# One two-bank tile for the scores of both attention halves, and three banks each for the other two groups

## The chip, the core and the metric

The kernel runs on one core of a Trainium2 chip. The metric is the device time of one execution in microseconds (us), lower is better. A profile of one execution is read beside it: TensorE is PE (its weight loads PEld), VectorE is DVE, ScalarE is ACT, GpSimd is POOL, and SP issues most transfers. L147 is line 147 of the kernel before.

## What is computed

One decoder block over 1024 tokens of width 1024 in float32. The part that the change touches is the sliding-window attention with sinks: 8 query heads and 2 key/value heads of width 64, blocks of 128 queries against the previous and their own 128 keys.

```python
s = jnp.einsum('bnqhgd,bnkhd->bnhgqk', qb, kk).astype(jnp.float32) * scale
...
s = jnp.where(valid[None, :, None, None], s, NEG_INF)
...
p = jax.nn.softmax(jnp.concatenate([s, sink], axis=-1), axis=-1)[..., :-1]
o = jnp.einsum('bnhgqk,bnkhd->bnqhgd', p.astype(v.dtype), vv)
```

Around it stand an input norm and projection (pool input, queries, keys, values, gates), a multi-scale pooling branch, gated merging, an output projection, and a squared-ReLU MLP with sandwich norms. The later stages are not changed.

## The kernel before

**Precision.** Each float32 operand is split into a high and a low part (`split`, L97: a cast on ACT at L98, a subtraction at L99, mostly on DVE), and each product is three matmuls: high x high, high x low, low x high (`PASSES`).

**Stages on PE, in order of time.** First the projections of queries, keys and values for token tiles 0 to 3, as x and the weights arrive (`mm_q` L147, `mm_kv` L153). Then eight one-column matmuls (L201) that end the sum of squares for the norm. Then the attention stage, tile by tile (n = 0 to 7): `qkv_tile(n + 4)` projects a later tile, 24 matmuls of 512 columns and 24 of 256; `pre_qkv` (L221, L222, on DVE) empties its banks, and rotates; `post_qkv` transposes queries and keys (L239, L240) and splits them; `score(n, g)` makes the scores of four heads; `attend(n, g)` makes their softmax, transposes it (L300), splits it (tiles "pt") and multiplies with the values (L307). Then the pooling branch: `pool_u` (48 matmuls of 512 columns for each of four groups, L345 and L347), `pool_in` on DVE, `pool_mix` (L518 to L520, evacuated at L521). Then the gates (`Pairs`, L408), and everything after.

**Scores.** In `score` the two key/value heads are two halves of 64 partitions each. Each of the 12 matmuls of a group (n, g) uses one half, so 64 of the 128 rows of PE. Each half has its own PSUM tile. Four reductions on DVE (L275) mask the scores and take their maxima.

**PSUM.** There are eight banks. One pool holds them in two groups of four, by tag: "at" (projections of tiles 0 and 1 at the start, transpositions, scores, products with the values) and "mm" (projections, pool_u, gates). All later stages use the same two tags.

**Order.** The engines run their instructions in the order that is built into the program. A scheduler makes that order when the program is built: by priority, which is by default the order in the source, and by whether a free buffer of the tag is there. So the projections of `qkv_tile` and the matmuls of `pool_u` stand between the steps of the attention.

Of the kernel before, what the change touches and what calls it, by code (L numbers as in the profile page):

```python
# [8 lines left out]
F32 = mybir.dt.float32  # L9
F32R = mybir.dt.float32r  # L10
AF = mybir.ActivationFunctionType
ALU = mybir.AluOpType
AX = mybir.AxisListType

P = 128
# [3 lines left out]
NK = D // P  # L19
# [4 lines left out]
HD = 64  # L24
# [7 lines left out]
PASSES = ((0, 0), (0, 1), (1, 0))  # L32
# [18 lines left out]
def block_kernel(ctx: ExitStack, tc, xt, x, consts, vecs, sinks, b_qkv, g_post, g_mlp, g_mlp_post,  # L51
                 w_qkv, w_u, w_g, w_pool, w_bp, w_ba, w_o, w_up, w_dn, x1_dram, spill, f_dram, out):
    nc = tc.nc
    act, dve, pool, pe = nc.scalar, nc.vector, nc.gpsimd, nc.tensor
# [3 lines left out]
    st = ctx.enter_context(tc.tile_pool(name="st", bufs=3))  # L58
    wp = ctx.enter_context(tc.tile_pool(name="wp", bufs=6))
    sp = ctx.enter_context(tc.tile_pool(name="sp", bufs=3))  # L60
    ps = ctx.enter_context(tc.tile_pool(name="ps", bufs=4, space=bass.MemoryType.PSUM))

    z_dram, y_dram, yp_dram = (spill[i:j] for i, j in ((0, 16), (16, 20), (20, 24)))
    cnt = [0]
# [1 line left out]
    def nm(s):  # L66
        cnt[0] += 1
        return f"{s}_{cnt[0]}"
# [13 lines left out]
    def at(tag, bufs, shape, dt=F32):  # L82
        return ap_.tile([P] + shape, dt, tag=tag, name=nm(tag), bufs=bufs)

    def bank(tag, shape=None):
        return ps.tile([P] + (shape or [512]), F32, tag=tag, name=nm(tag))

    def small(n=8, tag="sm"):
        return sp.tile([P, n], F32, tag=tag, name=nm(tag))
# [4 lines left out]
    def f32(ap):  # L94
        return ap.bitcast(F32)

    def split(hi, lo, src, eng=dve):  # L97
        act.copy(hi, src)  # L98
        eng.tensor_tensor(lo, src, f32(hi), ALU.subtract)  # L99
# [22 lines left out]
    nsnk = cp.tile([P, NH], F32, name="nsnk")  # L122
# [27 lines left out]
    def mm_kv(n, k, joint=False):  # L150

        for j, (xh, h) in enumerate(PASSES):
            pe.matmul(bkv[n // 2 * 2][:, n % 2, :], xs_[k][n // 4][:, xh, n % 4 * P:(n % 4 + 1) * P],  # L153
                      wkv[k // 2][:, h, k % 2, :], start=k == 0 and j == 0 and not (joint and n % 2),
                      stop=k == NK - 1 and j == 2 and not (joint and n % 2 == 0))

    bq = {0: bank("at"), 1: bank("at"), 2: bank("mm"), 3: bank("mm")}
    bkv = {0: bank("at", [2, 256]), 2: bank("mm", [2, 256])}
    bss = bank("at", [NT])
    sq = at("qkv", 2, [S])  # L160
    ones = vec[:, V_ONE:V_ONE + 1]
    for k in range(NK):
# [14 lines left out]
        kv = wkv[-1]  # L177
# [27 lines left out]
    khi = at("khi", 1, [S], F32R)  # L205
    klo = at("klo", 1, [S], F32R)
# [27 lines left out]
    def post_qkv(n):  # L234
        tf = tfs.pop(n)
        t = tf[:, :768].rearrange("p (h d) -> p h d", d=HD)
        bt, bk = bank("at"), bank("at")
        for m in range(4):
            pe.transpose(bt[:, m * P:(m + 1) * P], tf[:, m * P:(m + 1) * P], ident)  # L239
        pe.transpose(bk[:, :P], tf[:, 512:640], ident)  # L240
        qt = at("qt", 2, [2, 512], F32R)
        split(qt[:, 0, :], qt[:, 1, :], bt)
        ks = slice(n * P, (n + 1) * P)
        split(khi[:, ks], klo[:, ks], bk[:, :P])
        vt = at("v", 4, [2, 3, HD], F32R)
        pool.memset(f32(vt[:, :, 1, :]), 0.0)
        split(vt[:, 0, ::2, :], vt[:, 1, ::2, :], t[:, 10:12, :], pool)
        vs[n] = vt.rearrange("p l a d -> p l (a d)")
        qts[n] = qt
# [3 lines left out]
    def score(n, g):  # L253
        qt = qts[n]
        k0 = max(n - 1, 0) * P
        nk = 2 * P if n else P
        msk = mask[:, 2 * P - nk:]
        s4 = at("s4", 4, [4, 256])
        if g == 0:
            soft[n] = tuple(sp.tile([P, NH], F32, tag=t, name=nm(t)) for t in ("nmx", "es", "den"))  # L260
        nmx = soft[n][0]
        sb = [bank("at", [2, 256]) for _ in range(2)]
        for i in range(2):
            m = 2 * g + i
            for j, (qx, kx) in enumerate(((0, khi), (0, klo), (1, khi))):
                for kv in range(2):
                    r = slice(kv * HD, (kv + 1) * HD)
                    pe.matmul(sb[kv][:, i, :nk], qt[r, qx, m * P:(m + 1) * P], kx[r, k0:k0 + nk],  # L268
                              start=j == 0, stop=j == 2)

        for i in range(2):
            for kv in range(2):
                j = 2 * i + kv
                h = 4 * g + j
                dve.tensor_tensor_reduce(s4[:, j, :nk], sb[kv][:, i, :nk], msk, -HD ** -0.5, nsnk[:, h:h + 1],  # L275
                                         ALU.add, ALU.min, nmx[:, h:h + 1])
        scores[n, g] = s4

# [43 lines left out]
    rb = bcp.tile([P, 1024], F32, tag="bc", name="rb_all")  # L322
# [10 lines left out]
    def load_w(src, shape):  # L333
        ws = stage(shape)
        nc.sync.dma_start(ws, src)
        hi, lo = wslot(shape), wslot(shape)
        split(hi, lo, ws)
        return hi, lo

    def mm_fm(bs, whi, wlo, rhs, nk):  # L340

        for k in range(nk):
            for th in range(2):
                for hl in range(2):
                    pe.matmul(bs[th], whi[:, k, :], rhs(k, hl, th), start=k == 0 and hl == 0, stop=False)  # L345
            for th in range(2):
                pe.matmul(bs[th], wlo[:, k, :], rhs(k, 0, th), start=False, stop=k == nk - 1)  # L347

    def xr(k, hl, th):
        return xs_[k][th][:, hl, :]  # L350
# [96 lines left out]
    pre_qkv(0)  # L447
    pre_qkv(1)
    post_qkv(0)
    score(0, 0)  # L450
    score(0, 1)
    post_qkv(1)
    pre_qkv(2)
    pre_qkv(3)
    for n in range(NT):
        if n + 4 < NT:
            qkv_tile(n + 4)
        if n:
            score(n, 1)
        attend(n, 0)  # L460
        if n + 1 < NT:
            score(n + 1, 0)
        attend(n, 1)
        if n % 4 == 3:
            for kh in range(2):
                nc.sync.dma_start(y_dram[n // 4 * 2 + kh], flat(y[n // 4][kh]))
        if n == 1:
            make_rb()
        if n + 2 < NT:
            post_qkv(n + 2)  # L470
        if n + 4 < NT:
            pre_qkv(n + 4)
    us = {}

    def pool_u(gi):
        whi, wlo = load_w(w_u[gi], [NK, P])
        bs = [bank("mm"), bank("mm")]
        mm_fm(bs, whi, wlo, xr, NK)
        u = ga_.tile([P, S], F32, tag="ga", name=nm("u"))
        for th in range(2):  # L480
            sl = slice(th * 512, (th + 1) * 512)
            dve.tensor_tensor(u[:, sl], bs[th], rb[:, sl], ALU.mult)
        act.activation(u, u, AF.Identity, bias=vec[:, V_BU + gi:V_BU + gi + 1])
        us[gi] = u

# [10 lines left out]
    def pool_in(gi):  # L496
        w = WINDOWS[gi]
        u = us[gi]
        src, step = u, 1
        while step < w:  # L500
            t = flat(yy.tile([P, 2, 512], F32, tag="y", name=nm("t")))
            dve.tensor_tensor(t[:, step:], src[:, step:], src[:, :S - step], ALU.add)
            dve.tensor_copy(t[:, :step], src[:, :step])
            src, step = t, 2 * step
        dve.scalar_tensor_tensor(u[:, w - 1:], src[:, w - 1:], 1.0 / w, u[:, w - 1:], ALU.mult, ALU.subtract)
        dve.tensor_tensor(src[:, :w - 1], src[:, :w - 1], cst[:, C_CNT:C_CNT + w - 1], ALU.mult)
        dve.tensor_tensor(u[:, :w - 1], src[:, :w - 1], u[:, :w - 1], ALU.subtract)
        dhi, dlo = ar([S]), ar([S])
        split(dhi, dlo, u)
        d[gi] = dhi, dlo  # L510

    def pool_mix(gi):
# [9 lines left out]
        nc.scalar.dma_start(yp_dram[gi], yt)  # L522

    pool_u(3)
    pool_in(3)
    pool_u(2)
    pool_u(1)
    pool_mix(3)
    pool_in(2)
# [2 lines left out]
    pool_in(1)  # L532
    pool_in(0)
    ap_pool.__exit__(None, None, None)
    gp_pool = tc.tile_pool(name="gp", bufs=17, reuse_waits="tile")
    gp = gp_pool.__enter__()

# [84 lines left out]
    for p in range(8):  # L622
# [4 lines left out]
        tag = "at" if p % 2 == 0 else "mm"  # L627
# [276 lines left out]
    for p in range(1, NP):  # L904
# [3 lines left out]
        tag = "at" if p % 2 == 0 else "mm"  # L908
# [29 lines left out]
    def acc4(name):  # L938
        return [dl.tile([P, 512], F32, tag="acc", name=nm(name), bufs=16) for _ in range(4)]
# [82 lines left out]
    u, v, c11, c12 = acc4("u"), acc4("v"), acc4("c11"), acc4("c12")  # L1022
# [5 lines left out]
    for j, (i, s_) in enumerate(steps):  # L1028
        if j + AHEAD < len(steps):
            operands(*steps[j + AHEAD])  # L1030
        if s_ == 0 and i not in (2, 3):
            tag = "mm" if i in (5, 7) else "at"
            banks[i] = [bank(tag) for _ in range(4)]
        bs = banks[{2: 1, 3: 5}.get(i, i)]
# [104 lines left out]
```

## Time and profile before

| | us |
|---|---|
| three runs | 1170.08, 1171.26, 1171.52 |
| median | 1171.26 |
| the profiled execution, its own time | 1171.98 |
| its span | 1170.2 |
| PE busy | 1142.4 (98%) |
| DVE busy | 828.2 (71%) |
| ACT busy | 533.9 (46%) |

A row of matmuls gives their count, their busy time, and the mean length of one in ns. Matmuls are pipelined, so lengths overlap: what one costs is the busy time over the count, or the distance of two starts. The chain of waits follows the work that ended last back to its releasers. In the timeline the figure in brackets is the idle time of the engine before the row and what ended it.

### The profile page before, as it was taken

How to read it: one execution, taken by the hardware profiler on the slowest of the kernel's cores; microseconds unless marked ns; L12 is line 12 of the kernel's file. 1: busy time of each engine (PE TensorE's matmuls, PEld its weight loads, DVE VectorE, ACT ScalarE, POOL GpSimd, SP SyncE). 2: the span in 40 equal slices, each digit the busy share in tenths (PEclk: the TensorE clock that was granted, in tenths of full speed). 3: DMA queues.
4: the chain of work that ended last, by engine and by line, in shares of the span. 5: the costliest groups of instructions: out<-in, count | busy, mean ns of one | idle time of the engine just before them, and what ended most of it. 6: DMA issues, size and time to landing. Idle time of an engine off the chain costs nothing.

```text
span 1170.2 us, 14371 instructions
## 1 busy us (share of the span) xinstructions
PE 1142.4 (98%) x5356; PEld 942.4 (81%) x5356; DVE 828.2 (71%) x1337; ACT 533.9 (46%) x926; POOL 53.6 (5%) x66
## 2 busy tenths in 40 slices
PE   7999999999999999999999999999999999999995
PEld 6888888788888887888788888888878888888884
DVE  7767899888654585777988776666557945446795
ACT  6455655553432223465545444445344344444341
POOL 3411100000000140000000000000000000000000
PEclk9999999999999999999999999999999999999998
DMA  7102114554345444333255434343689654232852
GB/s 257 64 1 90 38 55 162 198 175 167 114 174 181 140 165 144 127 129 123 90 208 205 165 148 164 137 174 123 234 296 313 219 188 144 90 93 78 279 180 91
DMA packets 66167, 179.11 MB, mean 153 GB/s; under 512 B 6192, under 2 KB 6192, under 8 KB 66096
## 3 DMA queue, kind: packets, MB, share of 16 engines
q1 hardware_dynamic: 60480, 157.99, 39.0%
q10 hardware_dynamic: 5616, 20.19, 4.4%
q8 instruction: 42, 0.69, 0.2%
q14 instruction: 29, 0.24, 0.1%
HBM read 127.82 MB, written 50.33 MB: 152 GB/s over the span
## 4 chain that ended last, share of the span: by engine, by line
PE 89%; DVE 4%; DMA 3%; ACT 2%; issue 1%; SPq 0%; DVEq 0%; ACTq 0%
PE mm L408 21%; PE at L408 16%; PE at L998 13%; PE mm L998 11%; PE mm L345 7%; PE mm L719 5%; PE mm L347 4%; PE mm L147 3%; PE at L307 2%; PE at L268 2%; PE mm L153 1%; PE at L147 1%; PE at L300 1%; DMA B<-in_w_dn_dram 1%; DMA st<-in_w_up_dram 1%
## 5 line engine op out<-in xcount | busy, mean ns | idle before, releaser
L998 PE MATMUL at<-ar,wh 128*128 128x512 f32 x744 | 169.9, 389 | 0.9 <-DVE ar L99 0.5
L998 PEld LDWEIGHTS at<-ar,wh 128*128 128x128 f32 x744 | 139.5, 188 | 30.6 <-DVE ar L99 1.0
L99 DVE TENSOR_TENSOR wh<-raw,wh 128x1024 fp32r<-128x1024 f32 x53 | 64.9, 1225 | 94.0 <-ACT wh L98 94.0
L998 PE MATMUL mm<-ar,wh 128*128 128x512 f32 x576 | 131.0, 389 | 0.0
L98 ACT CAST wh<-st 128x512 fp32r<-128x512 f32 (+1 forms) x106 | 66.9, 641 | 131.5 <-PE mm L345 39.1
L998 PEld LDWEIGHTS mm<-ar,wh 128*128 128x128 f32 x576 | 108.2, 188 | 22.4
L98 ACT CAST wh<-raw 128x1024 fp32r<-128x1024 f32 x53 | 55.7, 1051 | 144.2 <-PE at L998 65.0
L99 DVE TENSOR_TENSOR wh<-st,wh 128x512 fp32r<-128x512 f32 (+1 forms) x106 | 82.9, 791 | 17.8 <-ACT wh L98 15.5
L408 PE MATMUL mm<-gr,wh 128*128 128x512 f32 x300 | 72.4, 391 | 0.1
L408 PE MATMUL mm<-T,wx 128*128 128x512 f32 x288 | 67.7, 389 | 0.0
L408 PEld LDWEIGHTS mm<-gr,wh 128*128 128x128 f32 x300 | 56.0, 188 | 12.0 <-ACT g L783 0.5
L408 PEld LDWEIGHTS mm<-T,wx 128*128 128x128 f32 x288 | 54.1, 188 | 11.2
L408 PE MATMUL at<-T,wx 128*128 128x512 f32 x252 | 59.1, 389 | 0.0
L408 PEld LDWEIGHTS at<-T,wx 128*128 128x128 f32 x252 | 47.3, 188 | 9.8
L408 PE MATMUL mm<-x,wh 128*128 128x512 f32 x216 | 51.5, 390 | 0.9 <-ACT g L415 0.9
L408 PEld LDWEIGHTS mm<-x,wh 128*128 128x128 f32 x216 | 40.4, 188 | 10.1 <-ACT g L415 1.7
L99 DVE TENSOR_TENSOR ar<-B,ar 128x1024 fp32r<-128x1024 f32 x37 | 45.2, 1221 | 1.0 <-ACT ar L98 0.9
L408 PE MATMUL at<-gr,wh 128*128 128x512 f32 x183 | 44.5, 390 | 0.0
L408 PE MATMUL at<-T,wh 128*128 128x512 f32 x153 | 40.9, 408 | 2.4 <-DVE f_first L434 2.2
L290 ACT ACTIVATE s<-s,nmx 128x256 f32<-128x256 f32 (+1 forms) x64 | 31.2, 493 | 25.8 <-DVE nmx L275 25.7
L644 DVE TENSOR_TENSOR g<-g,mm 128x512 f32<-128x512 f32 x32 | 20.6, 684 | 30.6 <-PE mm L347 30.6
L408 PEld LDWEIGHTS at<-gr,wh 128*128 128x128 f32 x183 | 34.3, 188 | 7.5 <-DVE wh L99 0.4
(332 smaller groups left out, 2296.2 us busy)
## 6 DMA issues: line engine op xcount, KB each, us to landing
raw<-f_dram SPq DMA_DIRECT2D x53, 512.0 KB, 3.7
f_dram<-g SPq DMA_DIRECT2D x30, 512.0 KB, 3.3
B<-in_w_dn_dram SPq DMA_DIRECT2D x24, 512.0 KB, 5.9
st<-in_w_up_dram SPq DMA_DIRECT2D x22, 512.0 KB, 3.6
f_dram<-g ACTq DMA_DIRECT2D x17, 512.0 KB, 2.6
st<-in_w_g_dram SPq DMA_DIRECT2D x16, 512.0 KB, 4.1
g<-spill_dram SPq DMA_DIRECT2D x16, 512.0 KB, 3.8
raw<-in_w_dn_dram SPq DMA_DIRECT2D x16, 512.0 KB, 4.7
```

The costliest lines, as they stand in the source:

```text
L98: act.copy(hi, src)
L99: eng.tensor_tensor(lo, src, f32(hi), ALU.subtract)
L147: pe.matmul(bq, xs_[k][n // 4][:, xh, n % 4 * P:(n % 4 + 1) * P], wq[k][:, h, :], start=k == 0 and j == 0, stop=k == NK - 1 and j == 2)
L268: pe.matmul(sb[kv][:, i, :nk], qt[r, qx, m * P:(m + 1) * P], kx[r, k0:k0 + nk], start=j == 0, stop=j == 2)
L290: act.activation(s4[:, j, :nk], s4[:, j, :nk], AF.Exp, scale=-1.0, bias=nmx[:, h:h + 1], accum_out=den[:, h:h + 1])
L307: pe.matmul(yb.rearrange("p m q -> p (m q)"), vs[k0 // P + kb][:, vh, kv * HD:kv * HD + P], pts[kv][:, ph, kb, :], start=j == 0, stop=j == ...
L345: pe.matmul(bs[th], whi[:, k, :], rhs(k, hl, th), start=k == 0 and hl == 0, stop=False)
L347: pe.matmul(bs[th], wlo[:, k, :], rhs(k, 0, th), start=False, stop=k == nk - 1)
L408: pe.matmul(b, w[:, wh, kt, :], xo[kt][:, xh, :], start=not after and kt == 0 and j == 0, stop=kt == 3 and j == 2, skip_group_check=after)
L644: dve.tensor_tensor(z[:, sl], z[:, sl], bs[th], ALU.mult)
L719: pe.matmul(obs[n][dj], l, wos[k][whl][:, dj * 512:(dj + 1) * 512], start=k == 0 and hl == 0 and whl == 0, stop=k == NK - 1 and hl == 1)
L998: pe.matmul(bs[t], fo[fh][:, k2, t * P:(t + 1) * P], wo_[wh][:, k2, :], start=not after and s2 == 0 and k2 == 0 and j == 0, stop=s2 == NS ...
```

## The change

The scores of both halves become one tile of two banks under a new tag "sc", with one buffer. The tags "at" and "mm" have three banks each during the attention and pooling stages; a second pool with four and four is opened behind them, for the gates and all after. The 12 matmuls of a score group are issued with high priority, so that the scheduler puts them in one run, with the order of the three passes turned: low key part first. The transpositions of `post_qkv` take their banks from "mm" in place of "at". The first two query projections use the score tile. `pool_u` does its two token halves one after the other, each in one bank, with the same 48 matmuls.

```diff
-    ps = ctx.enter_context(tc.tile_pool(name="ps", bufs=4, space=bass.MemoryType.PSUM))
+
+    psa_pool = tc.tile_pool(name="psa", bufs=1, space=bass.MemoryType.PSUM)
+    psum = {"pool": psa_pool.__enter__(), "bufs": {"sc": 1, "at": 3, "mm": 3}}
...
-        return ps.tile([P] + (shape or [512]), F32, tag=tag, name=nm(tag))
+        return psum["pool"].tile([P] + (shape or [512]), F32, tag=tag, name=nm(tag), bufs=psum["bufs"][tag])
...
-    bq = {0: bank("at"), 1: bank("at"), 2: bank("mm"), 3: bank("mm")}
+    bq01 = bank("sc", [2, 512])
+    bq = {0: bq01[:, 0, :], 1: bq01[:, 1, :], 2: bank("mm"), 3: bank("mm")}
...
-        bt, bk = bank("at"), bank("at")
+        bt, bk = bank("mm"), bank("mm")
...
-        sb = [bank("at", [2, 256]) for _ in range(2)]
-        for i in range(2):
-            m = 2 * g + i
-            for j, (qx, kx) in enumerate(((0, khi), (0, klo), (1, khi))):
-                for kv in range(2):
-                    r = slice(kv * HD, (kv + 1) * HD)
-                    pe.matmul(sb[kv][:, i, :nk], qt[r, qx, m * P:(m + 1) * P], kx[r, k0:k0 + nk],
-                              start=j == 0, stop=j == 2)
+        sb = bank("sc", [2, 2, 256])
+
+        with tc.high_priority():
+            for i in range(2):
+                m = 2 * g + i
+                for j, (qx, kx) in enumerate(((0, klo), (1, khi), (0, khi))):
+                    for kv in range(2):
+                        r = slice(kv * HD, (kv + 1) * HD)
+                        pe.matmul(sb[:, kv, i, :nk], qt[r, qx, m * P:(m + 1) * P], kx[r, k0:k0 + nk],
+                                  start=j == 0, stop=j == 2)
...
-                dve.tensor_tensor_reduce(s4[:, j, :nk], sb[kv][:, i, :nk], msk, -HD ** -0.5, nsnk[:, h:h + 1],
+                dve.tensor_tensor_reduce(s4[:, j, :nk], sb[:, kv, i, :nk], msk, -HD ** -0.5, nsnk[:, h:h + 1],
...
-        bs = [bank("mm"), bank("mm")]
-        mm_fm(bs, whi, wlo, xr, NK)
         u = ga_.tile([P, S], F32, tag="ga", name=nm("u"))
         for th in range(2):
             sl = slice(th * 512, (th + 1) * 512)
-            dve.tensor_tensor(u[:, sl], bs[th], rb[:, sl], ALU.mult)
+            b = bank("mm")
+            for k in range(NK):
+                for j, (xh, h) in enumerate(PASSES):
+                    pe.matmul(b, (whi, wlo)[h][:, k, :], xr(k, xh, th), start=k == 0 and j == 0,
+                              stop=k == NK - 1 and j == 2)
+            dve.tensor_tensor(u[:, sl], b, rb[:, sl], ALU.mult)
...
     ap_pool.__exit__(None, None, None)
+    psa_pool.__exit__(None, None, None)
+    psum["pool"] = ctx.enter_context(tc.tile_pool(name="ps", bufs=4, space=bass.MemoryType.PSUM))
+    psum["bufs"] = {"at": 4, "mm": 4}
```

## The prediction

> **What bounds the kernel now.** I read the page first (shares, slices, chain), then the windows of the first 200 us, the chain of waits in order of time, and last the timeline around single score groups. The page says that TensorE is the bound:
>
> ```profile
> span 1170.2 us, 14371 instructions
> PE 1142.4 (98%) x5356; PEld 942.4 (81%) x5356; DVE 828.2 (71%) x1337; ACT 533.9 (46%) x926; POOL 53.6 (5%) x66
> PE 89%; DVE 4%; DMA 3%; ACT 2%; issue 1%; SPq 0%; DVEq 0%; ACTq 0%
> L998 PE MATMUL at<-ar,wh 128*128 128x512 f32 x744 | 169.9, 389 | 0.9 <-DVE ar L99 0.5
> ```
>
> The last row also gives the price of a full matmul: 169.9 us for 744 is 0.228 us each (the 389 ns are its pipelined length). The windows give, per stretch, the busy time of PE, weight load, DVE, ACT and POOL, then the granted clock. The first three are about one clock period each, the last two are the attention stage:
>
> ```profile
> 41.45:44.86 3.41, 3.41 (x27) 3.12 (x26) 1.07 (x3) 1.05 (x2) 0.00 (x0) 1.00 0.11 42
> 44.86:48.28 3.42, 3.42 (x9) 2.68 (x9) 3.25 (x11) 0.30 (x1) 0.46 (x1) 0.50 0.00 0
> 48.28:51.69 3.41, 3.41 (x19) 2.81 (x18) 2.27 (x6) 0.75 (x2) 3.02 (x7) 1.00 0.00 0
> 57.00:110.00 53.00, 51.80 (x358) 44.38 (x357) 35.91 (x97) 28.06 (x92) 10.82 (x16) 1.00 0.08 26
> 110.00:175.00 65.00, 64.35 (x415) 53.46 (x414) 56.91 (x155) 40.84 (x124) 3.02 (x8) 1.00 0.18 62
> ```
>
> From 57 to 175 us PE is idle 1.2 + 0.65 = 1.85 us, so time can be won there only by giving PE less to do, and any new wait of PE is paid in full. DVE is busy 92.8 of 118 us, 79%: not the bound, but near.
>
> **The gain: paired score matmuls.** A score matmul uses 64 of the 128 rows. The chain shows the 12 matmuls of a group once alternating between the two halves, and twice in runs of one half:
>
> ```profile
> 73.08 0.91 PE at L268 x12
> 76.30 0.78 PE at L268 x5
> 78.58 0.90 PE at L268 x7
> 137.34 0.90 PE at L268 x6
> 139.75 0.90 PE at L268 x6
> ```
>
> Alternating, two run at once: 0.91 us. Split, they take 0.78 + 0.90 = 1.68 to 1.80 us. Eight of the 16 groups stand split in the chain (from 61, 76, 95, 112, 126, 137, 151 and 161 us). In the new issue order every group is one unbroken alternating run of 12, and the halves still lie in two banks (offset 512 of one tile). Gain: 8 x (1.74 - 0.91) = 6.6 us. Each run also pays for entering and leaving the 64-row mode:
>
> ```profile
> 75.90 0.40 PE L147 MATMUL mm<-wh,x 128*128 128x512 f32 x1
> 76.23 0.38 PE L268 MATMUL at<-khi,qt 64*128 64x256 f32 x1
> 79.40 0.96 PE L147 MATMUL mm<-wh,x 128*128 128x512 f32 x3
> 80.20 1.03 PE L300 MATMUL at<-cst,s 128*128 128x128 f32 x8
> ```
>
> One matmul ahead of a run holds PE 76.23 - 75.90 = 0.33 us instead of 0.228, three behind one hold it 0.80 instead of 0.68: 0.2 us a run. Eight groups in two runs become eight in one: 8 x 0.2 = 1.6 us more. Gain together: -8.2 us. The Trainium skill, "TensorEngine Tiling (Array Packing)", Gotcha 1, speaks against one tile for both halves: different row tiles must not write the same bank at the same time. By that rule a tile within one bank would bring none of these 8.2 us; no run shows such a tile, and here each half has its own bank, as before.
>
> **The first loss: no bank for the projections after the sum of squares.** Before, tag "mm" had four banks and bq[2], bq[3], bkv[2] held three, so the projection of tile 4 had the fourth and filled the wait for the norm. Now "mm" has three, all held, and the two banks of post_qkv's transpositions are also taken from "mm". In the new order the transpositions of tile 0 follow directly on the sum of squares (L201), and they wait for pre_qkv(2) on DVE to empty bq[2]:
>
> ```profile
> 42.31 1.95 PE L201 MATMUL at<-vec,qkv 128*128 128x1 f32 x16
> 44.12 5.97 PE L147 MATMUL mm<-wh,x 128*128 128x512 f32 x18
> 48.76 0.74 DVE L221 SCALAR_TENSOR_TENSOR y<-mm,r,bc 128x512 f32<-128x512 f32 x1
> 49.81 0.74 DVE L221 SCALAR_TENSOR_TENSOR y<-mm,r,bc 128x512 f32<-128x512 f32 x1
> 44.26 6.51 PE mm L147 x21
> ```
>
> DVE's order up to there is unchanged, so PE stands idle from 44.12 to 48.76 + 0.74 = 49.50: 5.4 us. Before, the same stretch ran at half clock (0.50 in the second window), where the 21 matmuls of the last row took 6.5 us in place of 21 x 0.228 = 4.8. That loss, 1.7 us, now falls on an idle engine: +5.4 - 1.7 = +3.7 us. What follows is not free either. The clock went to half for one 3.4 us window after a window of little work (the first). After 5.4 us of nothing it can stay at half through 51.7 or 55.1 us; about eight projections at half clock lose as many times 0.2 us, 1.6 us, at full clock none: I take +0.8. The Trainium skill, "TensorE: Matmul & The Clock Gate", Part 1, has it that an idle window of about 3.4 us halves the clock and a busy one restores it; by that the upper end would hold, and the row of 44.86 agrees with both halves of it.
>
> Then the head: the key transposition waits for the second bank (49.81 + 0.74 = 50.55), the next tile's for another, the scores now begin with the product on klo, which DVE makes last, and as "sc" has one buffer each following group waits for the four reductions of the one before:
>
> ```profile
> L275 DVE CUSTOM_DVE_ANT_0 s<-at,cst,nsnk 128x256 f32<-128x256 f32 x56 | 24.1, 481 | 11.8 <-PE at L268 11.6
> 55.09 0.63 PE L239 MATMUL at<-cst,qkv 128*128 128x128 f32 x4 [0.52 <-DVE nmx L275]
> 59.65 0.63 PE L300 MATMUL at<-cst,s 128*128 128x128 f32 x4 [1.20 <-DVE s L294]
> ```
>
> The 56 reductions keep DVE 24.1 us, 0.43 each, so a group is read in 1.7 us, of which the projections placed between hide about one: some 0.6 + 0.3 for the transpositions and 1.0 + 0.6 for two groups, 2.5 us, against the 0.52 + 1.20 that the last two rows have now, which go. +0.8, between 0 and 1.5.
>
> **The second loss: attends without cover.** Between the transpositions of a head group and its products stands a round over ACT and DVE, for both halves:
>
> ```profile
> L99 DVE TENSOR_TENSOR pt<-at,pt 128x512 fp32r<-128x512 f32 x28 | 18.0, 686 | 1.9 <-ACT pt L98 1.9
> L98 ACT CAST pt<-at 128x512 fp32r<-128x512 f32 x28 | 15.0, 585 | 7.6 <-PE at L300 7.5
> 73.92 1.09 PE L300 MATMUL at<-cst,s 128*128 128x128 f32 x8
> 74.77 0.95 PE L147 MATMUL mm<-wh,x 128*128 128x512 f32 x3
> 77.01 1.57 PE L307 MATMUL at<-pt,v 128*128 128x256 f32 x11
> ```
>
> One cast and two subtractions are 0.59 + 0.69 + 0.69 = 2.0 us from the first half's transpositions; PE's own work meanwhile is the other half's (0.5) and the products that are ready, about six of the 11 (0.8): 0.7 us uncovered, 0.9 with the hand-overs. Now projections (L147) and the next score group stand between L300 and L307, so little of it shows. In the new order scores have priority and use the projections as their cover; the attends of tiles 0 to 3 follow each other with two to five transpositions of post_qkv (0.1 us each) between, and four DVE reductions of the next group (1.7 us) can stand ahead of a subtraction. I charge eight attends 0.9 less a cover of 0.2, 5.6 us, and the other eight, which have pool_u as cover, what the stage has now. Against it goes about 0.6 us of the present 1.85: +5.0. All eight covered would be 0; eight more uncovered, or DVE late each time, +10. I take 5.0, near the middle, as the waiting rows of 59.65 and 55.09 show what happens where cover lacks.
>
> **The third loss: the change of pools.** The score tags end with the attention stage, and the first gate matmul waits until the old pool's last banks are read, that is for the second evacuation of pool_mix(2) (L521):
>
> ```profile
> 197.42 0.69 ACT L521 ACTIVATE u<-at,vec 128x512 f32<-128x512 f32 x1
> 197.90 5.60 PE L408 MATMUL mm<-x,wh 128*128 128x512 f32 x24
> 199.05 0.68 ACT L521 ACTIVATE u<-at,vec 128x512 f32<-128x512 f32 x1
> ```
>
> Now PE passes on to L408 at 197.90; it would have to wait for 199.05 + 0.68 = 199.73: +1.8 us (1.2 if ACT takes both evacuations together). DVE and ACT are then a little behind in the gate stage, 0 to 1.6, taken as +0.8.
>
> pool_u with one bank at a time issues the same 48 matmuls: nothing on PE, and its evacuation starts earlier. The initial bq[0], bq[1] in the score tile cost nothing, as the same DVE steps read them. On SP two loads and two stores of the attention stage change places; DMA is busy 0.18 there, so nothing. POOL's rotations are moved and are off the path.
>
> **The sum**: -8.2 + 3.7 + 0.8 + 0.8 + 5.0 + 1.8 + 0.8 = +4.7 us. The profiled run took 1171.98 us, 1.8 beyond its span, and lies 0.7 above the median 1171.26. So 1176.7 for such a run and 1176.0 for the median.
>
> **The rivals.** A measurement of this kernel can tell about 0.2% from no change, 2.3 us.
> - Faster: the attends are covered after all. The projections that the idle stretch displaced (4.8 us of work) are still to be issued, and where they fall into the waits the second loss is 0, as is the head's. For it: PE idles only 1.85 us in 118 now. Against it: the order, which places them in blocks ahead of the transpositions. -8.2 + 3.7 + 0 + 0 + 0 + 1.2 + 0 = -3.3: 1168.0. It decides where the waits behind 50 us, the pool change among them, add less than 8.2 - 3.7 - 2.3 = 2.2 us. Chance 0.12.
> - No change: they are covered by half, the second loss 2.0 in place of 5.0, and the gate stage is not behind: 4.7 - 3.0 - 0.8 = +0.9, 1172.2. Chance 0.15.
> - DVE becomes the bound: its 92.8 us must fit into a stage that is about 14 us shorter, as pool_u's work moves behind it; 92.8 of 104 is 89%, and all 16 attends wait. Second loss 10 in place of 5: 1181.0. Chance 0.09.
> - The clock stays at half into 58 us, as the stretch behind the gap is itself patchy: 1.6 to 3.2 us above the +0.8 taken, about 1178.4. Chance 0.06.
> - The pairs don't overlap when both halves lie in one tile: then the eight split groups gain nothing and the other eight become split, 2 x 6.6 = 13.2 us above the forecast, 1189.2. Separate banks speak against it. Chance 0.02.
> - The forecast, 1173.8 to 1178.2: 0.56.
>
> **The numbers.** Faster 0.12, same 0.15, slower 0.09 + 0.06 + 0.02 + 0.56 = 0.73. The range of 1169.6 to 1181.2 leaves out most of the first rival, the last, and half of DVE's: under 0.2. The forecast's own range is 1173.8 to 1178.2.
>
> **What would show it.** Right: all score groups in the chain at about 0.9 us for 12; PE without work from 44 to about 49.5 us and a granted clock of 0.5 beyond 48.3; PE waiting for the pt steps of ACT and DVE between 65 and 125 us; attention over some 10 us earlier, but the first L408 later than 197.9; from 260 us on the same rows at a constant shift. Wrong: PE work between 44 and 49 us, fewer than 3 us of PE waits in the attends, or a shift that arises behind 300 us.

## The result, and the profile after

| | before | after |
|---|---|---|
| median, us | 1170.57 (8 runs, 1168.37 to 1171.74) | 1177.66 (8 runs, 1175.12 to 1180.35) |
| the profiled execution, us | 1171.98 | 1179.32 |
| its span, us | 1170.2 | 1177.5 |

The ratio of the times is 1.0064, with a 95% interval of 1.0049 to 1.0078: the change makes the kernel 0.6% slower. The forecast was 1176.0 in a range of 1169.6 to 1181.2, with 0.73 for slower.

The page of the changed kernel, first lines (busy time, share of the span, instructions):

```profile
span 1177.5 us, 14366 instructions
PE 1141.1 (97%) x5356; PEld 941.3 (80%) x5356; DVE 827.7 (70%) x1337; ACT 535.1 (45%) x926; POOL 49.1 (4%) x66
```

PE is busy 1.3 us less than before (1142.4), although more of it runs at half clock, and idle 36.4 us in place of 27.8. So the gain is there, and idle time outweighs it. The windows of the changed kernel (columns as in the prediction: busy PE, PEld, DVE, ACT, POOL, then the granted clock):

```profile
44.86:48.28 3.42, 0.00 (x0) 0.00 (x0) 3.29 (x10) 0.30 (x1) 0.46 (x1) 0.54 0.00 0
48.28:51.69 3.41, 2.35 (x9) 1.61 (x9) 3.03 (x8) 1.55 (x5) 3.24 (x8) 0.50 0.00 0
51.69:55.10 3.41, 3.41 (x18) 2.70 (x17) 2.41 (x13) 1.58 (x3) 2.86 (x8) 0.50 0.03 5
55.10:58.52 3.42, 3.42 (x18) 2.38 (x16) 1.14 (x4) 2.21 (x10) 0.00 (x0) 0.50 0.01 2
58.52:61.93 3.41, 3.41 (x10) 2.43 (x8) 2.37 (x12) 1.75 (x9) 0.00 (x0) 0.50 0.00 0
```

The gap is empty, as forecast. But the clock stays at half for 17 us, from 45.1 to 62.2, also in three windows in which PE is busy all the time. What it costs is seen in the chain of waits (start, length, what), which also shows the score groups and the change of pools:

```profile
53.79 3.28 PE mm L149 x7
...
62.26 0.92 PE sc L273 x12
...
108.09 0.91 PE sc L273 x12
...
199.90 0.68 ACT u L529
200.58 1.04 ACT u L491
201.62 0.58 ACT u L529
202.25 5.76 PE mm L413 x24
```

Seven projections at half clock take 3.28 us, with a toll at both ends; their starts stand 0.427 us apart in place of 0.228. Behind 62 us each score group is one run of 12 in 0.91 to 0.92 us, the later tiles' too. And the first gate matmul (L413, L408 before) starts at 202.25 in place of 197.90, right behind the second evacuation (L529). PE's waits between 40 and 260 us name what it waits for (us in total, times, longest):

```profile
PE mm L242 <- DVE y L224: 5.3, 1, 5.3
PE mm L413 <- ACT g L420: 3.0, 1, 3.0
PE mm L413 <- ACT u L529: 1.8, 1, 1.8
PE at L312 <- DVE pt L101: 0.9, 3, 0.3
PE at L312 <- ACT pt L100: 0.6, 2, 0.3
PE at L305 <- DVE s L299: 0.2, 1, 0.2
```

Three waits stand out: the gap (L242 are the transpositions of `post_qkv`), the change of pools (L413 for u), and one in the gate stage (L413 for g) that the forecast had put much smaller.

For the comparisons below the stretch from 43.5 to 300 us is counted from matmul start to matmul start. Each distance is split into the slot of its shape (0.227 us for 512 columns, 0.119 for 256, 0.109 for 128), up to 0.11 us of toll beside a run of score matmuls, what half clock adds, and the rest, which is idle. A score matmul whose partner in the other half starts within 0.06 us shares one slot with it. "Score" is the slots of the score matmuls and the tolls. The last column but one is what the sum differs from before, the last how the medians differ, each from before in its own series of runs.

| kernel | score | half clock | idle 43.5-66 | idle 66-161 | idle 161-250 | profile - before | medians |
|---|---|---|---|---|---|---|---|
| before | 30.4 | 1.6 | 1.7 | 0.5 | 2.1 | | |
| changed | 21.2 | 5.9 | 7.0 | 4.2 | 5.2 | +7.2 | +7.1 |
| e1 runs only | 25.5 | 0 | 0 | 1.2 | 1.0 | -8.6 | -6.8 |
| e2 gap filled | 21.3 | 1.6 | 3.5 | 3.6 | 4.5 | -1.8 | +1.3 |
| e3 gap with junk (2.7 of junk) | 21.5 | 2.1 | 4.0 | 4.5 | 3.6 | +2.1 | +4.3 |
| e4 no priority | 26.6 | 8.1 | 7.0 | 6.2 | 7.3 | +18.9 | +18.6 |
| e5 pool by tile | 21.6 | 2.8 | 6.8 | 4.2 | 1.7 | +0.8 | +2.5 |
| e6 gate 3 first | 21.3 | 1.9 | 7.2 | 4.5 | 3.5 | +2.1 | +4.6 |
| e7 banks 2, 2, 4 | 22.8 | 2.9 | 1.9 | 1.5 | 5.3 | -1.9 | +1.5 |
| e8 priority alone | 25.8 | 0 | 0.2 | 1.4 | 0.9 | -8.0 | -7.2 |
| e9 e8, transpositions in mm | 26.1 | 3.1 | 6.7 | 4.1 | 0 | +3.7 | +5.2 |
| e10 e8, pool_u by halves | 26.4 | 0 | 0.2 | 1.2 | 1.2 | -7.3 | -7.2 |
| e11 e2 and e5 together | 21.4 | 1.4 | 3.7 | 3.7 | 1.4 | -4.7 | -5.3 |
| e12 transpositions in at | 23.1 | 2.8 | 7.9 | 3.1 | 3.8 | +4.4 | +6.5 |

What a run gains or loses against another is told below by the last column. A row is one execution, so single rows lie up to 3.4 us off the medians; part of that is the clock, as will be seen, and part is that the profiled execution of before (1171.98) lies 1.4 to 2.4 us above the medians of before. A row of a few us is a hint, a median a finding.

How a distance is divided between toll, half clock and idle time is partly a choice. With a toll allowed only on the distance across each end of a run and on the next one, before and changed kernel have 25.6 and 17.6 for score, 1.6 and 7.1 for half clock, and 2.7, 3.5, 3.1 and 6.2, 7.1, 5.6 for the three idle columns: +7.1 in sum again. So a difference in one column is good to about 2 us, while the sum is firm.

### The profile page after: what moved, and what is told of

Same layout as the page of the kernel before. It is cut to its first block, busy times and chain, and to the rows that moved or that the text cites. A ratio compares the mean times of both kernels' runs of the same rounds, so it can differ in the third digit from the quotient of the medians.

```text
span 1177.5 us, 14366 instructions
## 1 busy us (share of the span) xinstructions
PE 1141.1 (97%) x5356; PEld 941.3 (80%) x5356; DVE 827.7 (70%) x1337; ACT 535.1 (45%) x926; POOL 49.1 (4%) x66
## 4 chain that ended last, share of the span: by engine, by line
PE 82%; DVE 8%; DMA 4%; ACT 4%; issue 2%; SPq 0%; DVEq 0%; ACTq 0%
PE mm L413 19%; PE at L413 15%; PE at L1009 13%; PE mm L1009 11%; PE mm L350 5%; PE mm L488 4%; PE mm L730 3%; PE mm L149 3%; PE mm L352 2%; PE at L312 2%; PE sc L149 1%; DMA g<-in_w_up_dram 1%; PE sc L273 1%; PE mm L155 1%; DMA B<-in_w_dn_dram 1%
## 5 line engine op out<-in xcount | busy, mean ns | idle before, releaser
L413 PE MATMUL mm<-gr,wh 128*128 128x512 f32 x300 | 72.4, 391 | 0.1
L413 PE MATMUL mm<-T,wx 128*128 128x512 f32 x288 | 67.7, 389 | 0.0
L413 PEld LDWEIGHTS mm<-gr,wh 128*128 128x128 f32 x300 | 56.0, 188 | 12.0 <-ACT g L794 0.5
L413 PEld LDWEIGHTS mm<-T,wx 128*128 128x128 f32 x288 | 54.1, 188 | 11.2
L413 PE MATMUL at<-T,wx 128*128 128x512 f32 x252 | 59.1, 389 | 0.0
L413 PE MATMUL mm<-x,wh 128*128 128x512 f32 x216 | 53.1, 400 | 4.9 <-ACT g L420 3.0
L413 PEld LDWEIGHTS at<-T,wx 128*128 128x128 f32 x252 | 47.3, 188 | 9.8
L413 PEld LDWEIGHTS mm<-x,wh 128*128 128x128 f32 x216 | 41.4, 193 | 14.8 <-ACT g L420 3.7
L488 PE MATMUL mm<-x,wh 128*128 128x512 f32 x192 | 47.7, 393 | 0.0
L101 DVE TENSOR_TENSOR ar<-B,ar 128x1024 fp32r<-128x1024 f32 x37 | 45.1, 1220 | 0.6 <-ACT ar L100 0.4
L413 PE MATMUL at<-gr,wh 128*128 128x512 f32 x183 | 44.4, 389 | 0.0
L413 PE MATMUL at<-T,wh 128*128 128x512 f32 x153 | 41.0, 409 | 2.6 <-DVE f_first L439 1.9
L655 DVE TENSOR_TENSOR g<-g,mm 128x512 f32<-128x512 f32 x32 | 20.6, 684 | 30.4 <-PE mm L352 30.4
L488 PEld LDWEIGHTS mm<-x,wh 128*128 128x128 f32 x192 | 35.5, 188 | 6.5
```

The lines of the kernel that those rows point to most:

```text
L413: pe.matmul(b, w[:, wh, kt, :], xo[kt][:, xh, :], start=not after and kt == 0 and j == 0, stop=kt == 3 and j == 2, skip_group_check=after)
L488: pe.matmul(b, (whi, wlo)[h][:, k, :], xr(k, xh, th), start=k == 0 and j == 0, stop=k == NK - 1 and j == 2)
L655: dve.tensor_tensor(z[:, sl], z[:, sl], bs[th], ALU.mult)
```

## The experiments

**e1, the runs without the banks.** On the kernel before:

```diff
+        with tc.high_priority():
...
-                for j, (qx, kx) in enumerate(((0, khi), (0, klo), (1, khi))):
+                    for j, (qx, kx) in enumerate(((0, klo), (1, khi), (0, khi))):
...
```

> One part of the change alone, on the kernel before: the 12 score matmuls of a group are issued with priority and with the low key part first. The two score tiles, the four and four banks, the transpositions' tag, pool_u and the single PSUM pool stay as before. My theory is that the runs bring the gain and the banks bring most of the losses: score slots and mode tolls fall by about the 5.2 + 4.0 us that they fell in the changed kernel, the stretch behind the sum of squares has its projections again (no 5.3 us wait, no half clock beyond 48.3 us), the pool change is as before, and of the attends' extra 3.5 us of waits some part comes, as the order of the runs does that: 9 less 0 to 4, so 5 to 9 us below the kernel before. Rival one: priority itself does the harm, since a score group passes the projections that covered the attends; then 3 to 10 us of new waits in 66 to 161 us eat the gain, and the time is within 2 us of before. Rival two: without the common tile the two halves' groups do not stay together; then the rows of 12 score matmuls take about 1.7 us as in the split groups of before, and the time is at or above that of before.

1163.31 us, ratio 0.994 (0.9924 to 0.9956): faster than before. PE's waits from 40 to 260 us are all but gone:

```profile
PE mm L409 <- ACT g L416: 0.7, 1, 0.7
PE at L301 <- DVE s L295: 0.2, 1, 0.2
```

The runs are not perfect. Each half still waits for its own bank, and the chain shows groups in one run beside groups in two; many of the others take 1.04 to 1.32 us:

```profile
71.86 0.90 PE at L269 x6
...
73.65 0.90 PE at L269 x6
...
97.57 0.91 PE at L269 x12
```

So priority gives over half of the gain (30.4 to 25.5, against 21.2 with the common tile) and brings none of the losses. Rival one falls. Rival two holds for two groups of the chain, which still take 1.8 us in two runs of six (from 71.86 and 107.96 us), but not for the time.

**e8, priority alone.** As e1, with the passes in their old order (high x high first).

> The kernel before with priority for the score groups alone; the order of the three passes stays as it was (high x high first). It parts the two edits of the runs-only kernel. My theory: priority makes the runs and the order of the passes does little, so the time is within 2 us of the runs-only kernel's 1163. Rival: with high x high first the group starts before DVE has made the low key part, the run is split there and PE waits; then the rows of 12 score matmuls fall apart again and the time is 3 to 7 us above it, near the kernel before.

1162.33 us, 0.9935 (0.9923 to 0.9948): the order of the passes makes no difference that can be measured. With one added line this is faster than both kernels, and no other version is faster than it (e1 and e10 are within the noise of it). Its page:

```profile
PE 1135.1 (98%) x5356; PEld 938.8 (81%) x5356; DVE 826.6 (71%) x1337; ACT 533.5 (46%) x926; POOL 51.4 (4%) x66
```

Against before, PE is busy 7.3 us less in a span of 1160.1, and idle 25.0 in place of 27.8.

**e4, the banks without the runs.** On the changed kernel:

```diff
-        with tc.high_priority():
+        if True:
```

> The changed kernel without the priority of the score group: the common tile, the turned order of the passes and the banks stay. My theory is that the pairing comes of the priority: without it the scheduler puts projections and transpositions between the score matmuls again, some groups take 1.7 us in place of 0.92, and each switch between 64 and 128 rows costs its toll, so that up to 9 us of gain go, while the losses stay except for a part of the attends' 3.5 us: 3 to 9 us above the changed kernel. Rival: the common tile alone keeps the group in one run, as both halves' bank comes free at one time; then all groups still take 0.92 us and the time is within 1.5 us of the changed kernel.

1188.68 us, 1.0159 (1.014 to 1.0179): 11.5 us above the changed kernel, more than expected. The chain shows the groups in pieces:

```profile
84.87 0.55 PE sc L273 x5
...
86.92 0.66 PE sc L273 x7
```

The common tile keeps the halves alternating (12 matmuls cost 0.55 + 0.66 us), but not the group together: score slots are 11.9 us, near the changed kernel's 11.2, tolls 14.7 against 10.0. Waits grow too: 4.8 us at the change of pools, 1.7 more at the transpositions; by the table 5.4 of the row's 11.7 us are score, the rest half clock and idle time. So the two parts of the forecast's gain come mostly from two edits: the pairs from the common tile, the unbroken runs from the priority.

**e2, the gap filled.** The projections of token tile 4 get a bank that is free then:

```diff
-        bq[n] = bank("mm")
+        bq[n] = bank("at" if n == 4 else "mm")
```

> The changed kernel with one edit: the first projection bank of token tile 4 comes from the tag at, which is idle then, in place of mm, so that its 24 matmuls can start at 44 us while DVE still empties the three banks of mm. My theory: the 5.3 us wait between 43.8 and 49.3 us goes, and with it the half clock from 48.3 to 62.2 us (loss 4.4 us against 1.6 before); what the early projections then do not cover in the attends comes back, 1 to 3 us. So 4 to 7 us below the changed kernel, about 1172, at the time of before. Rival: the array merely does sooner what it would have done as cover later, and the waits in 66 to 161 us rise from 4.2 us by as much as the gap loses; then only the clock's 2.8 us are won, or less.

1171.35 us, 1.0006 (0.9992 to 1.0019): 5.8 us below the changed kernel, from one bank; the loss of the change is gone but for 1.3 us, which is within the noise. The timeline of PE shows projections (L149) where the changed kernel has none:

```profile
44.32 4.37 PE L149 MATMUL at<-wh,x 128*128 128x512 f32 x18
48.53 1.52 PE L149 MATMUL at<-wq,x 128*128 128x512 f32 x6
```

The clock is full through all windows from 41 to 62 us. Idle time in 66 to 161 us is 3.6, not more than the changed kernel's 4.2: the rival, that the early projections are then missing as cover, falls.

**e3, the gap filled with useless work.**

```diff
+    junk_b = bank("at")
+    for _ in range(12):
+        pe.matmul(junk_b, xs_[0][0][:, 0, :P], wq[0][:, 0, :], start=True, stop=True)
```

> The changed kernel with 12 added matmuls of 512 columns into a spare bank of at, issued behind the one-column matmuls of the sum of squares; nobody reads their result. They fill the first 3 to 5 us of the gap with work that brings nothing, so the gap stays as long as it is (DVE decides its end), but the array is not idle in the window 44.9 to 48.3 us. My theory, that the clock is a cost of its own which the idle window sets off: the granted clock is back at 1.0 by 51.7 us, the first score groups take 0.92 us in place of 1.47 and the projections 228 ns in place of 427, and 2.5 to 3 us are won. Rival: the clock stays at half because of what runs behind the gap (score matmuls on 64 rows, short transpositions), not because of the gap; then the windows of 51.7 to 62 us stay at 0.50, and the time is that of the changed kernel or up to 0.5 us above.

1174.34 us, 1.0034 (1.002 to 1.0047), 2.8 us below the changed kernel (1.0049 to 1.0078). PE has no more work that counts than there, so this fits a cost of the clock by itself. But the windows show that the way was not the one expected:

```profile
48.28:51.69 3.41, 1.13 (x5) 0.62 (x6) 3.41 (x10) 1.18 (x3) 2.47 (x7) 0.87 0.00 0
51.69:55.10 3.41, 3.40 (x20) 2.87 (x20) 2.15 (x9) 1.36 (x5) 3.41 (x10) 0.50 0.02 5
55.10:58.52 3.42, 3.42 (x20) 2.31 (x18) 1.18 (x10) 2.88 (x10) 0.23 (x1) 0.63 0.01 2
```

The junk moved the half clock from 45 to 50.8 us, behind what was left of the gap (2.4 us of wait), and shortened it from 17 to 6.8 us. It was not back by 51.7. Part of the 2.8 us may also be the gate stage, where this execution waited 1.6 us for g in place of 3.0, so how much of it the clock is stays open. The rival keeps a part as well: at half clock, what runs behind the gap has its say in how long that lasts, as the last section shows.

**e9 and e12, what empties the gap.** e9 is e8 with the transpositions of `post_qkv` in "mm", which keeps its four banks; e12 is the changed kernel with them back in "at", "mm" keeping three:

```diff
-        bt, bk = bank("at"), bank("at")
+        bt, bk = bank("mm"), bank("mm")
```

> The priority-alone kernel (four and four banks, 1162) with one further part of the change: the transpositions of post_qkv take their two banks from mm in place of at. It asks which of two things empties the array behind the sum of squares, the tag of the transpositions or the loss of mm's fourth bank. My theory, as the prediction put it first: the fourth bank is what the early projections need, so with four banks of mm they still run there, PE waits less than 1 us between 44 and 49.5 us, and the time stays within 2 us of 1162. Rival: the transpositions stand ahead of the projections of tile 4 in the order and take the place in mm that those had; then the 5.3 us wait is back although mm has four banks, with the half clock behind it, and the time is 5 to 10 us above 1162.

> The changed kernel with only the transpositions of post_qkv back in the tag at; the common score tile, three and three banks and all else stay. With the run that moves only their tag it parts the two causes of the gap behind the sum of squares. My theory: mm's three banks are held by bq[2], bq[3] and bkv[2], so even without the transpositions in mm nothing can run there; the 5.3 us wait stays, and the time is within 3 us of the changed kernel's. Rival: without the transpositions in mm the first bank that DVE empties goes to the projections at 46 to 47 us; then the wait is under 3 us, and 2 to 5 us are won.

e9: 1174.97 us, 1.0043 (1.0031 to 1.0055), 12.4 above e8 by this line alone. e12: 1176.25 us, 1.0056 (1.0044 to 1.0067), the changed kernel's time. PE's first waits, of e9 and then of e12:

```profile
PE mm L239 <- DVE qkv L232: 4.6, 1, 4.6
PE mm L239 <- POOL qkv L232: 2.3, 2, 1.8
```

```profile
PE at L242 <- DVE qkv L235: 4.6, 1, 4.6
PE mm L413 <- ACT u L529: 1.8, 1, 1.8
```

Either edit alone makes the gap. With four banks, the transpositions take the one that the projections had; with three, there is none for them. My theory fell for e9 (the rival's mechanism came, and cost more than the 5 to 10 us that it gave) and held for e12. In both PE stands at a transposition whose data come at 48.7 us anyway; what was lost is what ran meanwhile.

**e7, another division: score tile 2, "at" 2, "mm" 4**, transpositions in "at". The kernel of this run also leaves out `reuse_waits="tile"` at seven other pools, from that of x to the last, so it does not show the banks alone.

```diff
-    psum = {"pool": psa_pool.__enter__(), "bufs": {"sc": 1, "at": 3, "mm": 3}}
+    psum = {"pool": psa_pool.__enter__(), "bufs": {"sc": 1, "at": 2, "mm": 4}}
...
-    xpool = tc.tile_pool(name="xp", bufs=16, side="right", reuse_waits="tile")
+    xpool = tc.tile_pool(name="xp", bufs=16, side="right", )
...
-        bt, bk = bank("mm"), bank("mm")
+        bt, bk = bank("at"), bank("at")
...
-    gp_pool = tc.tile_pool(name="gp", bufs=17, reuse_waits="tile")
+    gp_pool = tc.tile_pool(name="gp", bufs=17, )
...
```

> The changed kernel with another division of the eight banks: the score tile has two, at has two in place of three, mm has four in place of three, and the transpositions of queries and keys go back to at. The projections behind the sum of squares then have their fourth bank, as in the kernel before. My theory: the wait of 5.3 us and the half clock behind it go (up to 9.7 us less 1.6), while the transpositions and the products with the values share two banks and wait more, 2 to 5 us beyond the 4.2 of the changed kernel, and the pool change and the gate stage stay as they are: 2 to 6 us below the changed kernel, so still not below the kernel before. Rival: three banks for at are not what the attends need, their waits come from DVE and ACT alone; then nothing is lost there and the time comes to 1169 or less.

1171.01 us, 1.0014 (1.0004 to 1.0024), in the range expected, but not by the way expected. The gap is filled; the attends with two banks do not wait more (1.5 us idle in 66 to 161 us, against 4.2). A price came at the change of pools and ahead of a score group:

```profile
PE mm L413 <- ACT u L529: 3.6, 1, 3.6
PE sc L273 <- ACT s L295: 1.5, 1, 1.5
```

Whether the banks or the pools that no longer wait by tile set the 3.6 us is not shown.

**e5, the second pool waits by tile.**

```diff
-    ...tc.tile_pool(name="ps", bufs=4, space=bass.MemoryType.PSUM))
+    ...tc.tile_pool(name="ps", bufs=4, space=bass.MemoryType.PSUM, reuse_waits="tile"))
```

> The changed kernel, with the second PSUM pool opened so that each of its tiles waits only for what lay in its own banks, and not for the whole first pool. In the changed kernel the first gate matmul (202.25 us) waits 2.3 us for the second evacuation of the last pool_mix. My theory of that loss, the pool change as such: the wait goes, the gates start about 2 us earlier, and the time falls by about 2 us. Rival: DVE and ACT are what is late there, so the array waits for the same evacuation a step later, or for the gates' own first evacuations; then a wait of 1.5 to 2.5 us stands at another line between 195 and 215 us, and the time changes by less than 0.7 us.

1172.11 us, 1.0026 (1.0016 to 1.0036): 4.6 us below the changed kernel, over twice what either side expected. The wait at the change of pools becomes a shorter one (L527), as the rival had it, but the one in the gate stage is nearly gone:

```profile
PE at L527 <- DVE ar L101: 1.1, 1, 1.1
...
PE mm L413 <- ACT g L420: 0.3, 1, 0.3
```

What the traces show as the reason is a load. In the gate stage DVE's sum of two operands (L386) stands ahead of steps that the array needs, and waits for a load of w_g. Timeline of the changed kernel (SP's issue, then DVE), and below of e5:

```profile
211.10 0.33 SPq L377 DMA_DIRECT2D st<-in_w_g_dram  x1
217.99 0.69 DVE L386 TENSOR_TENSOR ws<-st 128x512 f32<-128x512 f32 x1 [3.21 <-issue]
```

```profile
209.02 0.33 SPq L377 DMA_DIRECT2D st<-in_w_g_dram  x1
213.07 0.69 DVE L386 TENSOR_TENSOR ws<-st 128x512 f32<-128x512 f32 x1 [0.51 <-DVE gr L101]
```

Issued 2.1 us earlier, the sum runs 4.9 us earlier: 6.9 us from issue to use became at most 4.05. That the array waits for this load is borne out by the other traces: where it landed 6.8, 6.3, 5.3, 5.3, 4.0 and 3.6 us after its issue (changed kernel, e2, e3, e6, e5, e11), PE's wait for the evacuation that follows (L420 of the changed kernel) was 3.0, 2.5, 1.6, 1.5, 0.3 and 0 us. In the changed kernel five transfers of 512 KB were issued within 3.3 us around this load (209.39 to 212.74), in e5 within 5.0 (205.51 to 210.51), as the first stands 3.9 us earlier; e2 and e3 have the spacing of the changed kernel, e11 that of e5. So it looks as if the late change of pools bunches the transfers, and DVE's queue passes their delay on to the array. The bunching is argued, as no run moves the transfers alone, and at the same spacing the load's time still varies from 5.3 to 6.8 us.

**e6, DVE's order in the gate stage.** `build_gate(3)` gets priority, so that its subtractions stand ahead of that sum.

```diff
-    build_gate(3)
+    with tc.high_priority():
+        build_gate(3)
```

> The changed kernel, with build_gate(3) given priority, so that its subtractions on DVE stand ahead of the operand sum that waits for the weights of a later gate. In the changed kernel that sum is queued ahead of them and waits until the load lands at 217.9 us; the array then waits 3.5 us for ACT at 225 us and afterwards runs at half clock for one window (1.5 us). My theory: it is DVE's order; the stall and the half clock go, 2 to 3.5 us below the changed kernel, and the shift between 223 and 247 us falls back to what it is at 208 us. Rival: ACT and DVE are behind anyway since they took over the pooling work later, and the array waits as long for another of their steps; then the time changes by less than 1 us.

1174.19 us, 1.0043 (1.0031 to 1.0056), 2.5 us below the changed kernel, as my theory had it, and yet not shown:

```profile
PE mm L413 <- ACT u L529: 1.8, 1, 1.8
PE mm L413 <- ACT z L420: 1.5, 1, 1.5
```

A wait of 1.5 us stays, and e3, in DVE's old order and with a load that is as quick (5.3 us), has 1.6 there. This execution also had 10.2 us at half clock in the head in place of 17.1, and in all 1.9 us of half-clock loss in place of 5.9. So nothing here speaks for the order; whether it brings anything stays open.

**e10, pool_u by halves**, on e8.

```diff
-        bs = [bank("mm"), bank("mm")]
-        mm_fm(bs, whi, wlo, xr, NK)
+        for th in range(2): b = bank("mm"); ... (the same 48 matmuls)
```

> The priority-alone kernel with another single part of the change: pool_u does its two token halves one after the other, each in one bank, with the same 48 matmuls. The prediction put it at nothing. My theory now: the halves' evacuations end later on DVE for the last group, so the pooling branch closes later behind the attention stage and the array waits 1 to 3 us for it between 195 and 212 us; 1163 to 1166. Rival: the same matmuls and evacuations in another order, the time within 1 us of 1162.

1162.57 us, 0.9941 (0.9929 to 0.9953), against e8's 1162.33: nothing, as the prediction put it; my later theory fell.

**e11, e2 and e5 together.**

> The changed kernel with two of the earlier edits together: the first projection bank of token tile 4 from the tag at (alone 1171.4), and the second PSUM pool that waits by tile (alone 1172.1). If the two losses are separate, as I hold, the gains add: 1177.7 - 6.3 - 4.4, or 1166 to 1169, a little below the kernel before, and what is left against the priority-alone kernel are the attends' waits of 3.6 us and the pooling branch. Rival: the pool edit's gain came from another place of the DMAs and DVE's steps against each other in the gate stage, which shifts again when the head is 6 us earlier; then it is within 2 us of the 1171.4 of the gap edit alone.

1164.54 us, 0.996 (0.9946 to 0.9973): the two gains add, and a little more, below the range expected: 12.4 us below the changed kernel, where 5.8 and 4.6 make 10.4. So the change with two lines more is 0.4% faster than the kernel before. What it has against e8 is seen in the page and the waits:

```profile
PE 1134.1 (98%) x5356; PEld 935.7 (80%) x5356; DVE 826.3 (71%) x1337; ACT 534.7 (46%) x926; POOL 50.0 (4%) x66
```

```profile
PE at L305 <- DVE s L299: 1.2, 2, 1.1
PE at L527 <- DVE ar L101: 1.2, 1, 1.2
```

PE is busy 1.0 us less than in e8 and idle 28.7 us in place of 25.0: the common tile wins over the two tiles on PE, and its two banks cost more elsewhere.

## Why the prediction was right, and where its terms were off

The direction came as forecast, the size near it (+7.1 us for +4.7), and most causes did. The terms, from the table and the counts behind it (us, changed less before):

| term | forecast | measured |
|---|---|---|
| paired scores | -6.6 | -5.2 (slots 16.4 to 11.2) |
| tolls of the 64-row runs | -1.6 | -4.0 (14.0 to 10.0) |
| the gap, less the half clock of before | +5.4 - 1.7 | +5.3 - 1.6 |
| clock stays at half | +0.8 | +4.4 |
| head | +0.8 | 0 |
| attends | +5.0 | +3.6 |
| change of pools | +1.8 | +1.3 (a wait of 1.8) |
| gate stage | +0.8 | +1.9 idle, +1.5 half clock |
| sum | +4.7 | +7.2 |

The first two rows belong together: the forecast read 0.91 and 1.74 us from rows that hold the tolls inside a run. Per run there are four distances with about 0.1 us more, and it counted the two outer ones: behind 110.97 us the matmul ahead takes 0.319 in place of 0.227, the first of the run 0.220, its last 0.205 (0.114 to 0.115 between), and the matmul behind it 0.340. Together the gain is 8.2 by the forecast, 9.2 by this table and 8.0 with the narrower toll.

- **The gap** was right in place, length and cause: 5.3 us, and e2 shows that one bank undoes it. The prediction named the three banks and the tag together; e9 and e12 show that each alone suffices.
- **The clock** is the term mis-sized most. The prediction let it stay at half through 51.7 or 55.1 us; it stayed through 62.2. The rival that had it last into 58 us was there, with 0.06, and was the truer one. The prediction had weighed the Trainium skill, "TensorE: Matmul & The Clock Gate", Part 1, by which a busy window restores the clock. Here the clock rose at 62.18 us; counted back from there in its own period of 3.41 us, PE was busy all through the periods from 51.94 and from 55.35 us, and neither restored it. So busy as the profile counts it is not enough, and the measurement decides. The row of 44.86 did not agree with both halves of the rule either: the window ahead of it shows PE busy 3.41 us, and yet the clock fell. The +4.4 is also one execution's: e5 and e6 have the same matmuls in the same order up to 259 us and lost 2.8 and 1.9 us to half clock in all, in place of 5.9.
- **The attends** were oversized, by 1.4 us. By its own mark (fewer than 3 us of PE's waits would be wrong) this step fails: the waits view names 0.9 + 0.6 + 0.2 us for them. From starts it is 4.2 us of idle time, 3.6 more than before; a wait shorter than the modelled length of the matmul ahead of it is not seen as idle. The charge of 0.7 us for eight attends went the right way; the cover was better.
- **The gate stage** was undersized for want of a mechanism: that DVE's queue stands behind a load, and hands its delay on, was not seen. Behind it the clock fell once more, from 229.4 to 232.8 us.
- **DVE as the bound** did not come: 37.15 + 54.96 busy us of 118, no more than before. In the changed kernel's windows:

```profile
57.00:110.00 53.00, 51.93 (x368) 44.38 (x368) 37.15 (x116) 26.43 (x94) 5.67 (x14) 0.95 0.00 1
110.00:175.00 65.00, 63.87 (x439) 54.19 (x438) 54.96 (x141) 42.35 (x121) 3.73 (x11) 1.00 0.32 114
```

- **The shift** of the same matmul is 6.97 us from 233 us to behind 400 us, constant as forecast, and 7.83 at the end. The 0.9 us between, a sign of being wrong by the prediction's own list, are not explained.

The errors cancel in part: by the table the gain was 1.0 us larger and head, attends and pools 2.7 smaller than forecast, the clock and the gate stage 6.2 larger. That the total lay near is partly luck.

## What to carry to other kernels

Before banks are moved to make one step better, list who uses the banks at that time: here one bank that the projections lost cost 5.8 us, and a scheduler's priority gave over half of the gain with no bank moved at all. An idle stretch can cost more than its length, as the clock stays at half behind it, and a stage that starts late can move its loads against each other. Undo a bundled change part by part: its parts here are worth from -7 us (e8) to +12 (the line that parts e9 from e8).

## What the runs showed of the hardware

- **Half clock after an idle stretch of about 5 us lasts 10 to 17 us, not one window.** From 44 to 47 us on it lasted 17.1 us in the changed kernel and e4, 13.7 in e5 and e9, 10.2 in e6 and e12. In the changed kernel, e5 and e6 the matmuls of this stretch are the same in the same order, so the length differs from one execution to another. Windows of e12, where it ended soonest, to be held against those of the changed kernel:

```profile
48.28:51.69 3.41, 2.32 (x10) 1.92 (x11) 3.36 (x9) 1.25 (x4) 3.12 (x8) 0.50 0.00 0
51.69:55.10 3.41, 3.41 (x19) 2.51 (x19) 1.26 (x5) 1.05 (x3) 2.99 (x8) 0.56 0.02 5
55.10:58.52 3.42, 3.42 (x24) 2.63 (x23) 1.22 (x10) 3.03 (x10) 0.00 (x0) 1.00 0.01 2
```

  Windows with score matmuls on 64 rows among the projections restored the clock in e12 and not in the changed kernel; so neither busy time nor the 64 rows alone decide it. Counted in the clock's own periods (3.41 us, carried on from the changes of clock in each of the 14 traces, from 38 to 1100 us), a period at half clock that held only full matmuls, with 3584 columns or more, restored it all 23 times; one with score matmuls among them and 3200 columns or more did so 4 of 10 times. What decides there stays open.
- **The clock fell by the columns that a period held, not by busy time.** Of the periods at full clock with up to 2560 columns of matmuls started, 19 of 20 were followed by half clock, of those with 2831 to 3088 columns 8 of 14, and of 4276 with 3584 or more none. At 0.227 us for 512 columns about 7680 fit. So one and the same wait can cost a period at half clock or nothing: a wait of 1.8 us at the change of pools did so in e12 (3072 columns in its period, from 198.04 us) and not in the changed kernel (3072, from 198.71 us).
- **A load of 512 KB landed 5.3 to 6.8 us after its issue** where five such transfers were issued within 3.3 us (changed kernel, e2, e3), and 4.0 and 3.6 us after it where they were issued within 5.0 (e5, e11).
- **Pairing and runs are two things.** 64-row matmuls of two halves overlap wherever they alternate, also in pieces (0.55 us for 5, 0.66 for 7); each piece pays its tolls of four times about 0.1 us anew (25 pieces before, 16 in the changed kernel, 32 in e4).
